# The state product of a chunked scan: one float32 matmul per chunk against three matmuls of two-part operands, issued in another order

## The chip, the cores and the metric

The kernel runs on one core of one Trainium2 chip. The metric is the device time of one launch in microseconds (us). Three runs of the kernel before took 2647.37, 2649.1 and 2652.85 us; the median is 2649.1 us.

## The reference

One layer of a hybrid trunk over 2048 positions of 1024 features: RMSNorm, one wide input projection, two token mixers (a gated short convolution, and a state-space mixer), an output projection with a residual, then a squared-ReLU MLP and a last RMSNorm. The change lies in the state-space mixer alone. It has 16 heads of 64 in 2 groups, and a state of 128 for each group. Cut to what matters, for one chunk of positions `l`, `s` and one group:

```python
a_cum = cumsum(dt * a_head)
y_diag = einsum(scores * exp(a_cum[l] - a_cum[s]), x * dt)        # inside the chunk
states = einsum("ln,lrp->rpn", b, x * dt * exp(a_cum[-1] - a_cum))   # what the chunk adds to the state
h0 = zeros
h_next = h * exp(a_cum[-1]) + states                               # from chunk to chunk
y_off = einsum("ln,rpn->lrp", c, h_before) * exp(a_cum)            # what the state adds to the chunk
y = y_diag + y_off
```

The first chunk reads a state of zeros, and the state after the last chunk is read by nobody. After it come a skip term (`d_skip * x`), a gate (`silu(z)`) and a grouped RMSNorm.

## The kernel before

All large products (input projection, output projection, MLP) are float32-like: each operand is split into two float32r parts, `hi` (ScalarE copies and rounds) and `lo` (VectorE subtracts), and a product is three matmuls, `hi*hi`, `hi*lo` and `lo*hi`, into one PSUM bank (`mm3`, lines 111 to 114, and the same three in `Seven.chain`, lines 269 to 271). The big projections use a two-by-two scheme of seven block products.

The scan (class `Scan`) uses chunks of 128 positions: 4 blocks of 512 positions, 2 groups, 4 chunks each, so 32 chunks in the order of `CHUNKS`. They are numbered 0 to 31 here; the first chunks of the two groups are 0 and 4, the last ones are 27 and 31. Its work is woven into two stages of large products: chunks 0 to 15 into the second half of the input projection (`Proj.second_half`, profile 480 to 980 us), chunks 16 to 31 into the output projection (`Output.unit`, profile 980 to 1290 us). Each chunk has a `front` and a `back`, both generators, and `run` (the one who sets the order in which the source issues them) takes pieces of `back(n)` and of `front(n + 1)` in turn, one piece at each hook of the large stage.

The front, in three pieces: TensorE transposes the four x tiles into a PSUM bank (`ptx`, line 1227) and B into another (`ptb`, line 1229), and multiplies B by C into the rest of that bank (line 1230). ScalarE copies them out (`xtok` line 1232, `btok` line 1234), and VectorE masks the scores (`smask`, line 1236). Then ScalarE makes the decay table `dec` of the chunk, eight Relu passes (line 1241), which wait for the load of `dec` from DRAM, and one Exp over 1024 columns (line 1242); four passes scale the x tiles by `d_skip` (`xd`, line 1244), and VectorE makes `xdt` and `xde`, x times dt and x times the decay to the end of the chunk (line 1247). Last, VectorE multiplies `dec` by the masked scores (line 1249).

The back: TensorE multiplies the state by C (`yo`, four matmuls, line 1261), then B by `xde` (`st`, one float32 matmul of 128 by 512, line 1263), then eight matmuls for the heads (`yd`, line 1266). VectorE updates the state (lines 1274, 1275), adds the parts (1277, 1278, 1281), gates (1282), and ScalarE and VectorE form the norm (1285 to 1296).

The order on each engine is not the source's alone: a scheduler reorders the instructions of all engines by readiness and by its own estimates when the kernel is built. The order rows further down are what it has made. Each engine works through its own list in that order, and all DMA of the kernel is issued from SyncE's list, in its order. The PSUM tag `tp` has two banks that `ptx`, `ptb`, `st` and, in the first of the two stages, the norm's sum take in turn. `yo` and `yd` have one bank each. The temporaries of 512 columns (`stmp`) come from a ring of 3 tiles in the first stage and 4 in the second; the tables `dec`, `xd` and the loads have one tile in the first stage and two in the second.

Of the kernel before, what the change touches and what calls it, by code (L numbers as in the profile page):

```python
# [11 lines left out]
F32 = mybir.dt.float32  # L12
F32R = mybir.dt.float32r
AF = mybir.ActivationFunctionType
ALU = mybir.AluOpType

P = 128
# [3 lines left out]
NB = T // TB  # L21
L = 128
# [17 lines left out]
def trunk(ctx: ExitStack, tc: tile.TileContext, x, w_in, w_dt, w_out, w_up, w_down, cvec, hrow, out):  # L40
# [70 lines left out]
    def mm3(out, whi, wlo, hi, lo, k, nk):  # L111
        nc.tensor.matmul(out, whi, hi, start=(k == 0), stop=False)  # L112
        nc.tensor.matmul(out, whi, lo, start=False, stop=False)  # L113
        nc.tensor.matmul(out, wlo, hi, start=False, stop=(k == nk - 1))  # L114

    def psum(tag, name, bufs=1):
        if tag in turns:
            tag, bufs = next(turns[tag])
        return ps.tile([P, 512], F32, tag=tag, name=name, bufs=bufs)
# [1029 lines left out]
    class Scan:  # L1149
        def __init__(self, pool):  # L1150
            self.state = []
            for g in range(G):
                s0 = pool.tile([P, 512], F32, name=f"state{g}")
                nc.vector.memset(s0, 0.0)
                self.state.append(s0)
# [9 lines left out]
        def tmp(self):  # L1165
            return self.tile([512], "stmp", 2 + self.bufs)
# [6 lines left out]
        def load(self, n):  # L1173
# [20 lines left out]
            t["a"] = dd[:, 1, r0 : r0 + HG]  # L1194

        def load_rows(self, n):

            if n >= self.end:
                return
            b, g, c, h, ts, r0 = self.place(n)  # L1200
            if self.bufs == 1:
                eb = self.tile([4, L], "eb", 1)
            else:

                eb = uh.tile([P, 1, TB], F32R, tag="uh3", name="eb", bufs=4).bitcast(F32)
                eb = eb[:, 0].rearrange("p (j l) -> p j l", j=4)
            self.got[n]["eb"] = eb
            for hf in range(2):
                src = rd_d[b][r0 : r0 + HG, 1, :].rearrange("(j t) l -> t j l", t=2)[hf]
                nc.sync.dma_start(eb[hf * 64 : (hf + 1) * 64], src.partition_broadcast(64))  # L1210
# [7 lines left out]

        def front(self, n):
# [9 lines left out]
            nc.tensor.transpose(pb[:, 0:P], bT, ident)  # L1229
# [3 lines left out]
            btok = t["btok"] = self.tile([P], "btok", 1)  # L1233
            nc.scalar.copy(btok, pb[:, 0:P])
            sm = self.tile([L], "smask", 1)
            nc.vector.tensor_tensor(out=sm, in0=pb[:, P : 2 * P], in1=tri, op=ALU.mult)
            yield
# [7 lines left out]
            for k, by in (("xdt", "dt"), ("xde", "dend")):  # L1245
                t[k] = self.tmp()
                nc.vector.tensor_tensor(out=byhead(t[k]), in0=byhead(xtok), in1=t[by], op=ALU.mult)
# [4 lines left out]
        def back(self, n):  # L1252
# [6 lines left out]
            yo = psum("yo", "yo")  # L1259
            for j in range(4):  # L1260
                nc.tensor.matmul(yo[:, j * L : (j + 1) * L], state[:, j * P : (j + 1) * P], cT, start=True, stop=True)  # L1261
            st = psum("tp", "st", 2)
            nc.tensor.matmul(st, t["btok"], t["xde"], start=True, stop=True)  # L1263
# [10 lines left out]
            nc.vector.tensor_tensor(out=byhead(state), in0=byhead(state), in1=t["cdec"], op=ALU.mult)  # L1274
            nc.vector.tensor_tensor(out=state, in0=state, in1=st, op=ALU.add)
            t1 = self.tmp()
            nc.vector.tensor_tensor(out=t1, in0=yo, in1=t["eb"].rearrange("p j l -> p (j l)"), op=ALU.mult)
            nc.vector.tensor_tensor(out=t1, in0=t1, in1=yd, op=ALU.add)
            yield
            t3 = t1.rearrange("p (j l) -> p j l", j=4)  # L1280
            nc.vector.tensor_tensor(out=t3, in0=t3, in1=t["xd"], op=ALU.add)
# [10 lines left out]
            r = self.tile([L], "srstd", 1)  # L1292
# [342 lines left out]
```

## Time and profile before

| what | value |
|---|---|
| median of three runs | 2649.1 us (2647.37 to 2652.85) |
| the profiled execution, its own time | 2645.76 us |
| its span in the trace | 2643.8 us |
| TensorE busy (matmul) | 2596.8 us, 98% |
| VectorE busy | 1944.1 us, 74% |
| ScalarE busy | 1423.3 us, 54% |
| mean granted clock of TensorE | 0.997 |
| mean busy share of the DMA engines, 980 to 1100 us | 0.91 |
| mean busy share of the DMA engines, 1100 to 1265 us | 0.74 |

Times in the trace are microseconds from the start of the span. A row of the timeline gives start, duration, engine, line, operation, the tiles written and read, the shapes, how many instructions are merged into the row, and in brackets the idle time of the engine just before it with what ended it. A float32 matmul is two records in the trace (`yo` shows as x8 for four matmuls, `st` as x2 for one). Matmuls overlap, so what one costs is read from the starts of its neighbours, not from its own duration. The profiled execution is 3.3 us shorter than the median, and its span lies 2.0 us inside its own time.

### The profile page before, as it was taken

The page shows a single profiled execution, that of the slowest core. Times are in us where ns is not written, and L with a number is a line of the kernel's source. Part 1 is how long each engine was busy: PE and PEld are TensorE (multiplying, and loading weights), DVE is VectorE, ACT ScalarE, POOL GpSimd, SP SyncE. Part 2 cuts the span into 40 slices and gives each one's busy share as a digit, 9 for nine tenths or more (in the row PEclk, how much of TensorE's full clock was granted, in tenths as well). Part 3 has the DMA queues.
Part 4 walks back from the last instruction along what each step waited for, and adds up shares of the span by engine and source line. Part 5 has one row for each costly group of instructions (what it writes and reads, how often), then busy time and mean ns, then how long its engine had stood idle before and what let it go on. Part 6 is the DMA issues. An engine that isn't in the chain of part 4 may idle for free.

```text
span 2643.8 us, 33439 instructions
## 1 busy us (share of the span) xinstructions
PE 2596.8 (98%) x12026; PEld 2122.1 (80%) x12026; DVE 1944.1 (74%) x2650; ACT 1423.3 (54%) x2150; POOL 54.2 (2%) x98
## 2 busy tenths in 40 slices
PE   7999999999999999999999999999999999999998
PEld 5778888778878888888888888788887888888887
DVE  7997676767777777768767765755558877888885
ACT  6644345777567666666326555655555444444443
POOL 0000010000000000000000000000000000000001
PEclk9999999999999999999999999999999999999999
DMA  3585344655555478967666674744448554665762
GB/s 146 189 300 193 138 149 169 212 157 167 160 170 181 153 243 272 290 208 229 211 209 213 234 271 139 260 158 143 163 148 287 162 150 149 212 207 181 238 206 70
DMA packets 284806, 511.78 MB, mean 194 GB/s; under 512 B 25312, under 2 KB 141024, under 8 KB 284640
## 3 DMA queue, kind: packets, MB, share of 16 engines
q1 hardware_dynamic: 284640, 509.65, 58.5%
q8 instruction: 94, 1.54, 0.2%
q14 instruction: 72, 0.59, 0.1%
HBM read 344.41 MB, written 165.15 MB: 193 GB/s over the span
## 4 chain that ended last, share of the span: by engine, by line
PE 65%; issue 25%; DVE 3%; DMA 3%; ACT 3%; SPq 0%; POOL 0%; POOLq 0%; DVEq 0%; ACTq 0%
PE px L269 9%; PE px L271 9%; PE px L270 9%; PE pm L112 5%; PE pm L113 5%; PE pm L114 5%; PE py L269 4%; PE py L271 4%; PE py L270 4%; PE pw L269 2%; PE pw L271 2%; PE pw L270 2%; PE yd L1266 1%; PE st L1263 1%; PE yo L1261 1%
## 5 line engine op out<-in xcount | busy, mean ns | idle before, releaser
L269 PE MATMUL px<-uh,whi 128*128 128x512 f32 x1672 | 656.7, 393 | 11.7 <-ACT pw L277 4.8
L271 PE MATMUL px<-uh,wlo 128*128 128x512 f32 x1672 | 651.8, 390 | 1.8 <-DVE wlo L104 1.8
L270 PE MATMUL px<-ul,whi 128*128 128x512 f32 x1672 | 651.5, 390 | 0.0
L104 DVE TENSOR_TENSOR wlo<-wraw,whi 128x1024 fp32r<-128x1024 f32 x230 | 233.6, 1016 | 205.5 <-ACT whi L103 199.3
L269 PEld LDWEIGHTS px<-uh,whi 128*128 128x128 f32 x1672 | 314.0, 188 | 86.5 <-ACT pw L277 7.8
L271 PEld LDWEIGHTS px<-uh,wlo 128*128 128x128 f32 x1672 | 314.1, 188 | 68.9 <-DVE wlo L104 2.7
L270 PEld LDWEIGHTS px<-ul,whi 128*128 128x128 f32 x1672 | 314.2, 188 | 63.5
L103 ACT CAST whi<-wraw 128x1024 fp32r<-128x1024 f32 x230 | 203.4, 885 | 276.3 <-PE px L270 188.0
L103 ACT CAST whi<-s 128x1024 fp32r<-128x1024 f32 x210 | 219.6, 1046 | 234.3 <-PE pw L270 77.7
L269 PE MATMUL py<-uh,whi 128*128 128x512 f32 x836 | 327.3, 392 | 1.8 <-DVE acc L986 1.4
L270 PE MATMUL py<-ul,whi 128*128 128x512 f32 x836 | 325.4, 389 | 0.0
L271 PE MATMUL py<-uh,wlo 128*128 128x512 f32 x836 | 325.3, 389 | 0.0
L104 DVE TENSOR_TENSOR wlo<-s,whi 128x1024 fp32r<-128x1024 f32 x210 | 255.4, 1216 | 84.9 <-ACT whi L103 81.7
L112 PE MATMUL pm<-uh,whi 128*128 128x512 f32 (+1 forms) x648 | 252.6, 391 | 2.1 <-ACT uh L204 2.1
L113 PE MATMUL pm<-ul,whi 128*128 128x512 f32 (+1 forms) x648 | 248.9, 384 | 0.0
L114 PE MATMUL pm<-uh,wlo 128*128 128x512 f32 (+1 forms) x648 | 248.4, 383 | 0.0
L269 PEld LDWEIGHTS py<-uh,whi 128*128 128x128 f32 x836 | 156.9, 188 | 36.1 <-DVE acc L986 1.8
L271 PEld LDWEIGHTS py<-uh,wlo 128*128 128x128 f32 x836 | 156.8, 188 | 32.9
L270 PEld LDWEIGHTS py<-ul,whi 128*128 128x128 f32 x836 | 157.0, 188 | 32.2 <-issue 0.2
L269 PE MATMUL pw<-uh,whi 128*128 128x512 f32 x418 | 163.6, 391 | 0.7 <-ACT pw L277 0.7
L270 PE MATMUL pw<-ul,whi 128*128 128x512 f32 x418 | 163.0, 390 | 0.0
L319 ACT CAST uh<-rh 128x1024 fp32r<-128x1024 f32 (+1 forms) x128 | 120.4, 944 | 78.9 <-PE py L271 62.4
(226 smaller groups left out, 3710.6 us busy)
## 6 DMA issues: line engine op xcount, KB each, us to landing
hid_d<-e SPq DMA_DIRECT2D x96, 512.0 KB, 3.7
rh<-hid_d SPq DMA_DIRECT2D x96, 512.0 KB, 4.4
wraw<-w_in SPq DMA_DIRECT2D x68, 512.0 KB, 4.1
wraw<-w_up SPq DMA_DIRECT2D x64, 512.0 KB, 4.4
wraw<-w_down SPq DMA_DIRECT2D x104, 256.0 KB, 3.7
dec<-rd_d SPq DMA_DIRECT2D x32, 512.0 KB, 5.7
wraw<-w_out SPq DMA_DIRECT2D x32, 512.0 KB, 5.4
x_d<-xt SPq DMA_DIRECT2D x64, 256.0 KB, 3.8
```

The source lines that it names most:

```text
L103: nc.scalar.copy(hi, raw)
L104: eng.tensor_tensor(out=lo, in0=raw, in1=hi.bitcast(F32), op=ALU.subtract)
L112: nc.tensor.matmul(out, whi, hi, start=(k == 0), stop=False)
L113: nc.tensor.matmul(out, whi, lo, start=False, stop=False)
L114: nc.tensor.matmul(out, wlo, hi, start=False, stop=(k == nk - 1))
L269: nc.tensor.matmul(p, hi, h[0], start=bool(first and k == 0), stop=False, **kw)
L270: nc.tensor.matmul(p, hi, h[1], start=False, stop=False, **kw)
L271: nc.tensor.matmul(p, lo, h[0], start=False, stop=(k == len(g) - 1), **kw)
L319: nc.scalar.copy(p[i][0], t)
L1261: nc.tensor.matmul(yo[:, j * L : (j + 1) * L], state[:, j * P : (j + 1) * P], cT, start=True, stop=True)
L1263: nc.tensor.matmul(st, t["btok"], t["xde"], start=True, stop=True)
L1266: nc.tensor.matmul(yd[(i % 2) * 64 : (i % 2) * 64 + 64, (i // 2) * L : (i // 2 + 1) * L], byhead(t["xdt"])[:, i, :], t["dec"][:, i, :], st ...
```

## The change

The state product becomes an `mm3` of two-part operands: `btok` and `xde` are now pairs of float32r tiles which a new helper `pieces` makes (ScalarE rounds, VectorE subtracts). Both pairs are made in the first piece of the front, and so is `xdt`; `xde` is now x scaled in place in `xtok`. In the back, the state product stands ahead of the product of the state itself. The first chunk of each group has no product with the zero state, no load of its decay rows `eb` and no zeroed state; it copies `st` into the state. The last chunk of each group has no state product, no transpose of B and no update of the state. The norm's `srstd` is written over `ssq`, and the ring of temporaries has one tile less.

```diff
         def __init__(self, pool):
             for g in range(G):
-                s0 = pool.tile([P, 512], F32, name=f"state{g}")
-                nc.vector.memset(s0, 0.0)
-                self.state.append(s0)
+                self.state.append(pool.tile([P, 512], F32, name=f"state{g}"))
...
-            return self.tile([512], "stmp", 2 + self.bufs)
+            return self.tile([512], "stmp", 1 + self.bufs)
...
+            t["first"], t["last"] = (b, c) == (0, 0), (b, c) == (NB - 1, NC - 1)
 
         def load_rows(self, n):
...
+            if self.got[n]["first"]:
+                return
...
+        def pieces(self, shape, tag, src):
+
+            pair = self.sp.tile([P] + shape, F32R, tag=tag, name=tag, bufs=1)
+            hi, lo = pair[:, 0], pair[:, 1]
+            nc.scalar.copy(hi, src)
+            nc.vector.tensor_tensor(out=lo, in0=src, in1=hi.bitcast(F32), op=ALU.subtract)
+            return hi, lo
 
         def front(self, n):
...
-            nc.tensor.transpose(pb[:, 0:P], bT, ident)
+            if not t["last"]:
+                nc.tensor.transpose(pb[:, 0:P], bT, ident)
             nc.tensor.matmul(pb[:, P : 2 * P], bT, cT, start=True, stop=True)
             xtok = self.tile([512], "xtok", 1)
             nc.scalar.copy(xtok, pt)
-            btok = t["btok"] = self.tile([P], "btok", 1)
-            nc.scalar.copy(btok, pb[:, 0:P])
+            if not t["last"]:
+                t["btok"] = self.pieces([2, P], "btok", pb[:, 0:P])
             sm = self.tile([L], "smask", 1)
             nc.vector.tensor_tensor(out=sm, in0=pb[:, P : 2 * P], in1=tri, op=ALU.mult)
+            t["xdt"] = self.tmp()
+            nc.vector.tensor_tensor(out=byhead(t["xdt"]), in0=byhead(xtok), in1=t["dt"], op=ALU.mult)
+            if not t["last"]:
+                nc.vector.tensor_tensor(out=byhead(xtok), in0=byhead(xtok), in1=t["dend"], op=ALU.mult)
+                t["xde"] = self.pieces([2, 512], "xde", xtok)
             yield
...
-            for k, by in (("xdt", "dt"), ("xde", "dend")):
-                t[k] = self.tmp()
-                nc.vector.tensor_tensor(out=byhead(t[k]), in0=byhead(xtok), in1=t[by], op=ALU.mult)
             yield
...
-            yo = psum("yo", "yo")
-            for j in range(4):
-                nc.tensor.matmul(yo[:, j * L : (j + 1) * L], state[:, j * P : (j + 1) * P], cT, start=True, stop=True)
-            st = psum("tp", "st", 2)
-            nc.tensor.matmul(st, t["btok"], t["xde"], start=True, stop=True)
+            if not t["last"]:
+                st = psum("tp", "st", 2)
+                mm3(st, *t["btok"], *t["xde"], 0, 1)
+            if not t["first"]:
+                yo = psum("yo", "yo")
+                for j in range(4):
+                    nc.tensor.matmul(yo[:, j * L : (j + 1) * L], state[:, j * P : (j + 1) * P], cT, start=True, stop=True)
             yd = psum("yd", "yd")
...
-            nc.vector.tensor_tensor(out=byhead(state), in0=byhead(state), in1=t["cdec"], op=ALU.mult)
-            nc.vector.tensor_tensor(out=state, in0=state, in1=st, op=ALU.add)
             t1 = self.tmp()
-            nc.vector.tensor_tensor(out=t1, in0=yo, in1=t["eb"].rearrange("p j l -> p (j l)"), op=ALU.mult)
-            nc.vector.tensor_tensor(out=t1, in0=t1, in1=yd, op=ALU.add)
-            yield
             t3 = t1.rearrange("p (j l) -> p j l", j=4)
-            nc.vector.tensor_tensor(out=t3, in0=t3, in1=t["xd"], op=ALU.add)
+            if t["first"]:
+                nc.vector.tensor_copy(state, st)
+                yield
+                nc.vector.tensor_tensor(out=t1, in0=yd, in1=t["xd"].rearrange("p j l -> p (j l)"), op=ALU.add)
+            else:
+                if not t["last"]:
+                    nc.vector.tensor_tensor(out=byhead(state), in0=byhead(state), in1=t["cdec"], op=ALU.mult)
+                    nc.vector.tensor_tensor(out=state, in0=state, in1=st, op=ALU.add)
+                nc.vector.tensor_tensor(out=t1, in0=yo, in1=t["eb"].rearrange("p j l -> p (j l)"), op=ALU.mult)
+                nc.vector.tensor_tensor(out=t1, in0=t1, in1=yd, op=ALU.add)
+                yield
+                nc.vector.tensor_tensor(out=t3, in0=t3, in1=t["xd"], op=ALU.add)
...
-            r = self.tile([L], "srstd", 1)
+            r = ssq
```

Counted over the whole program, TensorE has 90 float32r matmuls of 128 by 512 for `st` in the place of 32 float32 ones, 120 instead of 128 for `yo`, and 30 instead of 32 transposes of B. VectorE has 30 more subtractions of 128 columns and 30 more of 512, and lacks two zeroings, and two or four each of the state's and the output's passes. ScalarE has 30 more casts of 512 columns and 86 instead of 89 table loads. SyncE has four loads fewer. Ahead of chunk 0 and behind chunk 31 the lists of all engines read alike.

The state product on TensorE, in chunk 5 (`st` is the state product, `yo` the product with the state, `yd` the heads). Before:

```order
L1261 MATMUL yo<-bc,state_3779 128x128 x4
L1263 MATMUL st<-stmp,btok 128x512
L1266 MATMUL yd<-dec,stmp 64x128 x8
```

And now:

```order
L112 MATMUL st<-xde,btok 128x512
L113 MATMUL st<-xde,btok 128x512
L114 MATMUL st<-xde,btok 128x512
L1277 MATMUL yo<-bc,state_3778 128x128 x4
L1280 MATMUL yd<-dec,stmp 64x128 x8
```

The group stays at the same place between the large matmuls in all middle chunks; inside it, the state product has come to the front.

ScalarE around the front of chunk 26, in the output projection. `xtok` and `btok` are this chunk's, while the `dec` rows and the Exp with its table load (L1242 before, L1257 now) are already those of the chunk after it; `stmp<-y` is the square of the norm, `whi` a weight of the projection. Before:

```order
L1285 ACTIVATE stmp<-y 128x512
L1241 ACTIVATE dec<-dec,dd 128x128 x4
L1244 ACTIVATE xd<-xd,cv 128x128
L1232 COPY xtok<-ptx 128x512
L1234 COPY btok<-ptb 128x128
L1244 ACTIVATE xd<-xd,cv 128x128 x3
L1241 ACTIVATE dec<-dec,dd 128x128 x4
L1242 ACT_TABLE_LOAD
L1242 ACTIVATE dec<-dec 128x1024
L103 CAST whi<-wraw 128x1024
```

And now:

```order
L1256 ACTIVATE dec<-dec,dd 128x128 x8
L1259 ACTIVATE xd<-xd,cv 128x128 x2
L1242 COPY xtok<-ptx 128x512
L1224 CAST btok<-ptb 128x128
L1305 ACTIVATE stmp<-y 128x512
L1259 ACTIVATE xd<-xd,cv 128x128 x2
L1257 ACT_TABLE_LOAD
L1257 ACTIVATE dec<-dec 128x1024
L1224 CAST xde<-xtok 128x512
L103 CAST whi<-wraw 128x1024
```

All eight passes over `dec` now stand ahead of the copy `xtok`, and the cast `xde`, which is new, stands behind the square, the table load and the Exp. VectorE at the same place, now:

```order
L1248 TENSOR_TENSOR stmp<-xtok,dd 128x512
L1225 TENSOR_TENSOR btok<-ptb,btok 128x128
L1246 TENSOR_TENSOR smask<-ptb,tri 128x128
L1250 TENSOR_TENSOR xtok<-xtok,dd 128x512
L1306 TENSOR_TENSOR stmp<-stmp 128x256
L1261 TENSOR_TENSOR dec<-dec,smask 128x1024
L1308 TENSOR_TENSOR ssq<-stmp 128x128
L1225 TENSOR_TENSOR xde<-xtok,xde 128x512
L1481 TENSOR_TENSOR xt<-pm,xt 128x512
```

The subtraction `xde`, the last thing that the state product needs, stands behind the product of `dec` with the scores. In chunks 25, 26 and 29 the Exp of the next chunk stands ahead of the cast `xde`; in 23, 24 and 30 it stands behind it.

ScalarE ahead of the Exp of chunk 2, in the input projection. Before:

```order
L717 ACT_TABLE_LOAD
L717 ACTIVATE ea<-pw 128x512
L651 ACT_TABLE_LOAD
L651 ACTIVATE dts<-pr 64x128
L1232 COPY xtok<-ptx 128x512
L725 ACT_TABLE_LOAD
L725 ACTIVATE eb<-eb 128x512
L1234 COPY btok<-ptb 128x128
L1293 ACT_TABLE_LOAD
L1293 ACTIVATE srstd<-pss,cv 128x128
L731 ACT_TABLE_LOAD
L731 ACTIVATE ea<-ea 128x512
```

And now:

```order
L651 ACTIVATE dts<-pr 64x128
L1242 COPY xtok<-ptx 128x512
L1256 ACTIVATE dec<-dec,dd 128x128
L1224 CAST btok<-ptb 128x128
L1313 ACT_TABLE_LOAD
L1313 ACTIVATE ssq<-pss,cv 128x128
L725 ACT_TABLE_LOAD
L725 ACTIVATE eb<-eb 128x512
L1224 CAST xde<-xtok 128x512
L731 ACTIVATE ea<-ea 128x512
```

Three of the five table loads of this stretch are gone, since the passes that share a table now stand together; one pass over `dec` and the cast `xde` have come in.

## The prediction

> **What bounds the kernel now.** I read the page first, then the busy time by stretches, then the timeline of each engine around single chunks.
>
> ```profile
> PE 2596.8 (98%) x12026; PEld 2122.1 (80%) x12026; DVE 1944.1 (74%) x2650; ACT 1423.3 (54%) x2150; POOL 54.2 (2%) x98
> 1100.00:1265.00 165.00, 164.42 (x879) 132.51 (x878) 121.61 (x186) 100.50 (x198) 0.00 (x0) 1.00 0.74 226
> ```
>
> TensorE is the bound, and in the second scan stage, too (second row: 164.4 of 165 us busy, granted clock 1.00; VectorE 121.6, ScalarE 100.5). So every microsecond that TensorE need not work comes off the end, as long as nothing makes it stand. The first half of my sum is its work, the second half its standing.
>
> The work of one chunk stands between large matmuls. Chunk 4 has all three products, chunk 3 `st` and `yd` alone, chunk 12 `yo` and `st` alone:
>
> ```profile
> 611.46 0.39 PE L271 MATMUL py<-uh,wlo 128*128 128x512 f32 x1
> 611.69 1.05 PE L1261 MATMUL yo<-bc,state 128*128 128x128 f32 x8
> 612.58 1.02 PE L1263 MATMUL st<-stmp,btok 128*128 128x512 f32 x2
> 613.53 1.09 PE L1266 MATMUL yd<-dec,stmp 128*64 128x128 f32 x16
> 614.90 0.40 PE L270 MATMUL px<-ul,whi 128*128 128x512 f32 x1
> ...
> 583.78 0.40 PE L271 MATMUL pw<-uh,wlo 128*128 128x512 f32 x1
> 584.01 1.02 PE L1263 MATMUL st<-stmp,btok 128*128 128x512 f32 x2
> 586.32 0.39 PE L270 MATMUL px<-ul,whi 128*128 128x512 f32 x1
> ...
> 841.82 0.39 PE L271 MATMUL px<-uh,wlo 128*128 128x512 f32 x1
> 842.93 1.02 PE L1263 MATMUL st<-stmp,btok 128*128 128x512 f32 x2
> 844.02 0.40 PE L270 MATMUL py<-ul,whi 128*128 128x512 f32 x1
> ```
>
> A large float32r matmul takes 0.39 us by its own row, yet the next starts 0.23 us after it (611.46 to 611.69). Each group lies between two large matmuls with a third inside, so its cost is the distance from the first row to the last, less two times 0.23: 2.98 us for all three products, 2.08 for `st` and `yd`, 1.74 for `yo` and `st`. By differences `yo` costs 0.89 and `st` 0.85; by its start and the start behind it (612.58 to 613.53) `st` costs 0.95. These are the bounds, 0.85 and 0.95.
>
> **The change, part by part: TensorE's work.** Three float32r matmuls of the shape of the large ones cost 3 x 0.23 = 0.69 us. So a chunk saves 0.16 to 0.26 us, and 30 chunks 4.8 to 7.8 us; I take 6. Two first chunks lose `yo` (2 x 0.89 = 1.8), two last ones `st` (2 x 0.85 = 1.7) and a transpose each (an eighth of `yo`'s 0.89, so 0.2 together). Sum: 9.7 us, bounds 8.5 and 11.5.
>
> The Trainium skill ("FP8 and Floating Point Precision", TensorE Precision Notes) says that true float32 goes through the array in four passes, and the reduced form reads a truncated operand. By that rule `st` costs 4 x 0.23 = 0.91 us as an estimate, and the 30 chunks save 6.6 us instead of 6; the rows agree within their bounds.
>
> **A stall that goes.** In chunk 2 TensorE stands 1.66 us ahead of `yd`, because the Exp of the decay table is late on ScalarE:
>
> ```profile
> 552.14 1.28 ACT L1242 ACT_TABLE_LOAD   x1
> 553.44 1.06 ACT L1242 ACTIVATE dec<-dec 128x1024 f32<-128x1024 f32 x1
> ...
> 556.02 1.09 PE L1266 MATMUL yd<-dec,stmp 128*64 128x128 f32 x16 [1.66 <-DVE dec L1249]
> ```
>
> The new ScalarE list has three table loads fewer ahead of this Exp (3 x 1.28 = 3.8 us) and about 1 us of new passes, so the Exp comes 2.8 us sooner. I take 1.5 us of gain, bounds 0 and 1.7.
>
> **New waits on TensorE.** The state product now needs a longer chain: `xtok` copied (ScalarE), scaled (VectorE), rounded (ScalarE), subtracted (VectorE). It also stands first in its group, so the 0.89 us of `yo` no longer hide anything, and `yo`, `yd` and all large matmuls queue behind it. The Trainium skill ("PSUM — Partial Sum Buffer", Engine vs sequencer instructions) says the same of all lists: ScalarE and VectorE are strict first-in first-out, and matmuls start in order. By that rule a late part costs its full lateness; with overtaking it would cost nothing, and the sum would be 11.2 us of gain.
>
> In the input projection the chain has room: in chunk 12, the tightest of 4 to 15, `xde` is ready at 834.3, 7.7 us ahead of `yo` at 842.04 (0.89 ahead of the `st` above). In the output projection it has not, since ScalarE itself stands, waiting for the load of the next chunk's `dec` (seven times from 1100 to 1250 us). The rows are chunk 12's `xde`, that wait, and chunk 26:
>
> ```profile
> 833.60 0.68 DVE L1247 TENSOR_TENSOR stmp<-xtok,dd 128x512 f32<-128x512 f32 x1
> ...
> ACT dec L1241 <- DMA dec<-rd_d: 21.0, 7, 4.5
> ...
> 1160.81 1.28 ACT L1241 ACTIVATE dec<-dec,dd 128x128 f32<-128x128 f32 x4 [3.94 <-DMA dec<-rd_d]
> 1162.29 0.56 ACT L1232 COPY xtok<-ptx 128x512 f32<-128x512 f32 x1
> 1162.76 0.26 ACT L1234 COPY btok<-ptb 128x128 f32<-128x128 f32 x1
> 1162.91 0.99 ACT L1244 ACTIVATE xd<-xd,cv 128x128 f32<-128x128 f32 x3
> 1163.80 1.27 ACT L1241 ACTIVATE dec<-dec,dd 128x128 f32<-128x128 f32 x4
> 1165.09 1.28 ACT L1242 ACT_TABLE_LOAD   x1
> 1166.39 1.06 ACT L1242 ACTIVATE dec<-dec 128x1024 f32<-128x1024 f32 x1
> 1167.35 1.03 ACT L103 CAST whi<-wraw 128x1024 fp32r<-128x1024 f32 x1
> ...
> 1162.89 0.69 DVE L1247 TENSOR_TENSOR stmp<-xtok,dd 128x512 f32<-128x512 f32 x1 [4.56 <-ACT xtok L1232]
> 1163.50 0.28 DVE L1236 TENSOR_TENSOR smask<-ptb,tri 128x128 f32<-128x128 f32 x1
> 1163.70 0.68 DVE L1247 TENSOR_TENSOR stmp<-xtok,dd 128x512 f32<-128x512 f32 x1
> 1164.30 1.22 DVE L1249 TENSOR_TENSOR dec<-dec,smask 128x1024 f32<-128x1024 f32 x1
> ...
> 1166.28 1.05 PE L1261 MATMUL yo<-bc,state 128*128 128x128 f32 x8
> ```
>
> From start to start a `dec` or `xd` pass takes 0.30 us, a copy of 512 columns 0.47 (so I take the square and the cast at 0.5), `btok` 0.15, the table load 1.30, the Exp 0.96; on VectorE 0.60 for 512 columns, 0.20 for 128, 1.13 for 1024. The new list, from the landing at 1160.81: eight `dec` 2.4, two `xd` 0.6, `xtok` 0.5, `btok` 0.15, square 0.5, two `xd` 0.6, table 1.3, Exp 1.0, cast 0.5: the `hi` part is ready at 1168.4, `lo` 0.65 later at 1169.0. TensorE comes at 1166.28 and needs `lo` for its second matmul, 0.23 us on: it stands 2.5 us. The other four tight chunks go the same way from their own copy of `xtok`:
>
> ```profile
> 1125.04 0.56 ACT L1232 COPY xtok<-ptx 128x512 f32<-128x512 f32 x1
> 1128.20 1.05 PE L1261 MATMUL yo<-bc,state 128*128 128x128 f32 x8
> ...
> 1143.72 0.58 ACT L1232 COPY xtok<-ptx 128x512 f32<-128x512 f32 x1
> 1148.61 1.05 PE L1261 MATMUL yo<-bc,state 128*128 128x128 f32 x8
> ...
> 1220.49 0.56 ACT L1232 COPY xtok<-ptx 128x512 f32<-128x512 f32 x1
> 1222.05 1.05 PE L1261 MATMUL yo<-bc,state 128*128 128x128 f32 x8
> 1223.68 1.10 PE L1263 MATMUL st<-stmp,btok 128*128 128x512 f32 x2 [0.58 <-DVE stmp L1247]
> ...
> 1238.58 0.56 ACT L1232 COPY xtok<-ptx 128x512 f32<-128x512 f32 x1
> 1240.60 1.05 PE L1261 MATMUL yo<-bc,state 128*128 128x128 f32 x8
> ```
>
> In chunks 24 and 30 the Exp is behind the cast, and VectorE sets the end: from the end of the copy `xdt` 0.6, `btok` and `smask` 0.4, `xtok` 0.6, the half-sum 0.4, `dec` 1.13, the subtraction 0.65, in all 3.8: 0.9 us of standing in 24, 2.0 in 30. In chunk 25 nine `dec` and `xd` passes, square, table and Exp come first: 6.8 us from the copy's end, 2.2 us of standing. In chunk 29 it is 5.3 us, 4.0 of standing, of which 0.74 is there before (1222.05 + 0.89 to 1223.68): 3.3 new. Chunk 28 has the wait behind its copy, and 27 and 31 have no state product. Sum: 0.9 + 2.2 + 2.5 + 3.3 + 2.0 = 10.9 us, and 0.5 for chunks 0 and 16, whose products the list puts close behind their parts.
>
> Not all of it need come. While TensorE stands, SyncE's list and the transfers go on, so after a stall the next `dec` lands sooner as TensorE sees it; and the list has one load fewer ahead of some `dec` loads. I take 9 us, bounds 2 and 14 (above the sum, if VectorE's longer list makes the loads later).
>
> **What I cost at nothing.** The 30 x (0.2 + 0.6) us more on VectorE and 30 x 0.5 on ScalarE beyond these waits lie under TensorE (121.6 and 100.5 of 165 us busy); without that cover they would be 39 us. The state's update now waits for `yo` 0.69 us later on VectorE, under the same cover, since the next pass waits for `yd` anyway. The passes, loads and zeroing left out in first and last chunks gain as little. The smaller ring has each tile's last reader done ahead of its next writer.
>
> **Sum.** -9.7 - 1.5 + 9 = -2.2 us on the profiled span of 2643.8 us (2645.76 us by its own time, 3.3 under the median of 2649.1). On the median: 2646.9 us. Its own range, from the bounds: -11.5 - 1.7 + 2 = -11.2 to -8.5 + 14 = +5.5.
>
> **Rivals.** First, the waits do not come: the new order lets the `dec` loads land early enough that ScalarE no longer stands ahead of `xtok`. For it: SyncE's new list puts `dec` ahead of a load or store in three of these chunks. Against it: the wait is there seven times, 3.94 us in chunk 26. Then 0 to 3 us of waits are left: -11.2 + 2 = -9, 2640 us. Second, slower: VectorE, 0.8 us a chunk longer, evicts the units of the projection later, their stores go out later, and SyncE, in order, issues each `dec` that much later. This decides from about 0.5 us of delay a chunk on, and adds 0.8 us in each of six tight chunks (23 to 26, 29, 30) to the uncorrected 11.4: -11.2 + 11.4 + 4.8 = +5, or with chunk 28 drawn in +6: 2655 us. Third, the change does not do what it says: the matmuls of `st` take the 0.39 us of their rows each and not 0.23. Then `st` costs 1.17, 0.32 more than now, and the 30 chunks lose 9.6 us where I have a gain of 6: 2662.5 us. The large matmuls of the same shape, 0.23 apart, speak against it.
>
> **Chances.** The sum as it stands, 0.55 (2646.9); waits that mostly do not come, 0.30 (2640); late loads, 0.12 (2655); the third, 0.03 (2662.5). Two runs of this kernel differ by about 0.2%, 5.3 us, so that much is what a measurement can tell. Faster than 2643.8: most of the second case and a fifth of the first, 0.37. Slower than 2654.4: the last two and little of the first, 0.16. Between: 0.47. Range for 8 in 10: 2637 to 2654.
>
> **What would show it.** Right: `st` rows 0.23 apart at the head of each group and groups 0.16 to 0.26 us shorter; no wait at `yd` in chunk 2; TensorE standing 1 to 4 us ahead of the second or first `st` matmul in chunks 24, 25, 26, 29 and 30 with VectorE's `xde` as the releaser, and ScalarE waiting for `dec` ahead of `xtok`. Wrong: no standing there (then 2640), or standing in chunks 17 to 22 too, where I give 1.5 us of room and more.

## The result, and the profile after

The changed kernel took 2640.7 us (median of eight runs, 2636.3 to 2643.9); the kernel before, run beside it, 2647.5 us. The ratio is 0.998, with a 95% interval of 0.9971 to 0.9989: between 3 and 8 us faster, 5.3 us by the middle (the two medians lie 6.8 apart). The profiled execution took 2640.53 us, and its span went from 2643.8 to 2638.8 us. The forecast was 2646.9 us. The time lies inside the range, but at the number of my first rival, 2640; the range is wide enough to hold both.

The page's row of busy times, the stretch of the second scan stage by windows (start to end, length, then busy time of TensorE, its weight loads, VectorE, ScalarE and GpSimd, the granted clock, the DMA share and GB/s), and TensorE's waits from 470 to 1320 us (total, times, longest):

```profile
PE 2588.8 (98%) x12034; PEld 2127.0 (81%) x12034; DVE 1955.7 (74%) x2696; ACT 1432.9 (54%) x2175; POOL 58.2 (2%) x98
...
1100.00:1265.00 165.00, 161.90 (x872) 133.07 (x871) 122.66 (x195) 104.11 (x204) 0.00 (x0) 1.00 0.76 230
...
PE st L112 <- ACT xde L1224: 1.6, 2, 1.2
PE pss L1311 <- ACT xtok L1242: 1.5, 2, 0.7
PE ptx L1236 <- DMA xd<-xs_d: 1.4, 3, 0.6
PE st L113 <- DVE xde L1225: 1.3, 4, 0.6
```

TensorE works 8.0 us less in all, but in the second stage it is no longer busy throughout: it stood 0.58 us there before and 3.10 now. Two kinds of wait are new: `st` for the parts of `xde`, and the norm's sum `pss` for the copy of `xtok`.

A chunk without a wait, from TensorE's timeline (chunk 5):

```profile
636.94 0.40 PE L271 MATMUL px<-uh,wlo 128*128 128x512 f32 x1
637.17 0.39 PE L112 MATMUL st<-xde,btok 128*128 128x512 f32 x1
637.40 0.39 PE L113 MATMUL st<-xde,btok 128*128 128x512 f32 x1
637.63 0.40 PE L114 MATMUL st<-xde,btok 128*128 128x512 f32 x1
637.86 1.06 PE L1277 MATMUL yo<-bc,state 128*128 128x128 f32 x8
638.85 1.09 PE L1280 MATMUL yd<-dec,stmp 128*64 128x128 f32 x16
639.87 0.50 PE L269 MATMUL py<-uh,whi 128*128 128x512 f32 x1
640.20 0.39 PE L270 MATMUL py<-ul,whi 128*128 128x512 f32 x1
```

The three matmuls of the state product start 0.23 apart. From the first row to the last, less two times 0.227, the group costs 2.815 us; it was 2.979. Both are medians over the groups that hold these three products, so a chunk saves 0.164 us.

Chunk 25 is the longest wait. First TensorE, then ScalarE's list ahead of it:

```profile
1144.52 0.39 PE L114 MATMUL pm<-uh,wlo 128*128 128x512 f32 x1
1146.16 0.49 PE L112 MATMUL st<-xde,btok 128*128 128x512 f32 x1 [1.25 <-ACT xde L1224]
1146.88 0.50 PE L113 MATMUL st<-xde,btok 128*128 128x512 f32 x1 [0.23 <-DVE xde L1225]
```

```profile
1137.49 0.99 ACT L1256 ACTIVATE dec<-dec,dd 128x128 f32<-128x128 f32 x3 [6.65 <-DMA dec<-rd_d]
1138.39 1.03 ACT L103 CAST whi<-wraw 128x1024 fp32r<-128x1024 f32 x1
1139.32 0.58 ACT L1242 COPY xtok<-ptx 128x512 f32<-128x512 f32 x1
...
1142.25 0.98 ACT L1256 ACTIVATE dec<-dec,dd 128x128 f32<-128x128 f32 x3
1143.24 1.28 ACT L1257 ACT_TABLE_LOAD   x1
1144.54 1.06 ACT L1257 ACTIVATE dec<-dec 128x1024 f32<-128x1024 f32 x1
1145.50 0.60 ACT L1224 CAST xde<-xtok 128x512 fp32r<-128x512 f32 x1
```

ScalarE stands 6.65 us for the `dec` of chunk 26, while the copy of chunk 25's `xtok` stands behind it; then the rest of chunk 26's Relu passes, the table load and the Exp go ahead of the cast of `xde`. TensorE comes at 1144.75 and gets `hi` at 1146.1.

The kernel has 10,890 matmuls outside the scan, as many in every version. I set the k-th of one trace against the k-th of the other; the difference of their starts shows where time is won and lost. The whole gaps between them show waits more fully than the idle times in brackets: the stall of chunk 2 is 1.66 us in brackets and 2.1 by its gap. In us, against the kernel before (negative is earlier):

| place in the kernel before | the change |
|---|---|
| 468.6 us (scan not begun) | -0.8 |
| 563.9 us (chunk 2 done) | -4.5 |
| 971.8 us (first stage nearly done) | -3.7 |
| 1103.7 us (chunk 22 done) | -5.1 |
| 1159.0 us (chunk 25 done) | -2.0 |
| 1274.2 us (scan done) | -4.2 |
| 2633.4 us (end) | -4.6 |

So the scan is worth 3.4 us of the 5.0; the rest lies in stages that the change doesn't touch, where two executions of one kernel differ as much (experiments 5 and 11 run the same kernel; at 468.6 us one is 1.1 us ahead of the kernel before, the other 0.7 behind). The gains come at the first chunks and the last ones. Between chunk 2 and chunk 22 the cheaper products (20 x 0.164) and the `yo` that chunk 4 lacks (0.89) should give 4.2 us and leave 0.6: waits of `pss` take 2.0, chunk 3's `yo`, which stood ahead of the mark at 563.9 and now stands behind it, 0.9, and the other 0.7 is spread over waits of large products and transposes. Chunks 23 and 25 take 3.5.

### The profile page after: what moved, and what is told of

Read it like the earlier page. It is cut to its first block, busy times and chain, and to the rows that moved or that the text cites. A ratio compares the mean times of both kernels' runs of the same rounds, so it can differ in the third digit from the quotient of the medians.

```text
span 2638.8 us, 33504 instructions
## 1 busy us (share of the span) xinstructions
PE 2588.8 (98%) x12034; PEld 2127.0 (81%) x12034; DVE 1955.7 (74%) x2696; ACT 1432.9 (54%) x2175; POOL 58.2 (2%) x98
## 4 chain that ended last, share of the span: by engine, by line
PE 65%; issue 25%; DMA 4%; DVE 3%; ACT 3%; SPq 0%; POOL 0%; POOLq 0%; DVEq 0%; ACTq 0%
PE px L269 9%; PE px L271 9%; PE px L270 9%; PE py L269 5%; PE py L271 4%; PE py L270 4%; PE pm L112 4%; PE pm L113 4%; PE pm L114 4%; PE pw L269 2%; PE pw L271 2%; PE pw L270 2%; DMA dec<-rd_d 1%; PE yd L1280 1%; PE yo L1277 1%
## 5 line engine op out<-in xcount | busy, mean ns | idle before, releaser
L271 PE MATMUL pw<-uh,wlo 128*128 128x512 f32 x418 | 162.9, 390 | 0.0
```

The costliest lines, as they stand in the source:

```text
L271: nc.tensor.matmul(p, lo, h[0], start=False, stop=(k == len(g) - 1), **kw)
```

## The experiments

Theory A: the change saves about 8.6 us of TensorE's work and a stall of 1.66, and loses part of it because the parts of `xde` come late in the second stage, behind the next chunk's `dec` on ScalarE. Theory B: the two-part product is worth nothing here in any case, and the gain comes from the rest. The last five columns are the same differences of starts, in us, at the places of the table above:

| kernel | median us | ratio to before, 95% | 563.9 | 971.8 | 1103.7 | 1159.0 | 1274.2 |
|---|---|---|---|---|---|---|---|
| the change | 2640.7 | 0.998 (0.9971 to 0.9989) | -4.5 | -3.7 | -5.1 | -2.0 | -4.2 |
| 1 float32 product, first | 2641.9 | 0.9985 (0.9976 to 0.9994) | -4.7 | -4.0 | -3.1 | -3.1 | -5.9 |
| 2 state's own product first | 2646.9 | 1.0004 (0.9993 to 1.0016) | -0.3 | -2.5 | -3.0 | +0.6 | -2.5 |
| 4 ends only | 2645.4 | 0.9994 (0.9981 to 1.0007) | -0.9 | -1.1 | +0.4 | +0.6 | +2.3 |
| 5 Relu held behind | 2636.1 | 0.9959 (0.9945 to 0.9973) | -4.1 | -4.3 | -5.1 | -5.5 | -8.6 |
| 6 the same, float32 product | 2641.7 | 0.9989 (0.998 to 0.9999) | -5.4 | -5.1 | -1.7 | -1.4 | -4.2 |
| 7 parts late in the source | 2638.4 | 0.9977 (0.9968 to 0.9986) | -3.5 | -4.5 | -3.9 | -1.9 | -2.9 |

**1. The two-part operands undone alone.** `btok` and `xde` are plain float32 tiles, made at the same place:

```diff
-                t["btok"] = self.pieces([2, P], "btok", pb[:, 0:P])
+                btok = t["btok"] = self.tile([P], "btok", 1)
+                nc.scalar.copy(btok, pb[:, 0:P])
...
-                nc.vector.tensor_tensor(out=byhead(xtok), in0=byhead(xtok), in1=t["dend"], op=ALU.mult)
-                t["xde"] = self.pieces([2, 512], "xde", xtok)
+                t["xde"] = self.tile([512], "xde", 1)
+                nc.vector.tensor_tensor(out=byhead(t["xde"]), in0=byhead(xtok), in1=t["dend"], op=ALU.mult)
...
-                mm3(st, *t["btok"], *t["xde"], 0, 1)
+                nc.tensor.matmul(st, t["btok"], t["xde"], start=True, stop=True)
```

> The changed kernel with the two-part operands undone alone: the state product is one float32 matmul again, still first in its group, and xde and btok are plain float32 tiles made in the first piece. In the two traces a middle chunk went from 2.979 to 2.815 us, so 30 chunks should get 30 x 0.164 = 4.9 us longer. The chain ahead of the product gets shorter by a cast (0.5) and a subtraction (0.65). Theory A (the parts' lateness causes the new waits, 1.4, 1.9, 0.8 and 0.5 us in chunks 23, 25, 29 and 30): these 4.6 us mostly go, and the sum is 2640.7 + 4.9 - 4.6 = 2641, no difference from the changed kernel. Theory B (the waits come from the late decay load alone, whatever the operands are): the waits stay, 2645.6.

Measured: 2641.9 us, which the runs can't tell from the change. TensorE's timeline of chunk 5, and its one wait from 1090 to 1265 us:

```profile
635.57 1.02 PE L1274 MATMUL st<-xde,btok 128*128 128x512 f32 x2
636.43 1.05 PE L1278 MATMUL yo<-bc,state 128*128 128x128 f32 x8
637.41 1.09 PE L1281 MATMUL yd<-dec,stmp 128*64 128x128 f32 x16
...
PE ptb L1239 <- DVE state L1298: 1.0, 1, 1.0
```

Here `st` costs 0.86 us (635.57 to 636.43), and the groups have a median of 2.985 us. No wait at `st` is left, so the waits belong to the longer chain of the two-part operands, as A said. But the price stands too: as the change was built, the waits ate what the cheaper product saved (by the two traces the float32 version is even 1.7 us ahead at the end of the scan).

**2. The order undone alone.**

```diff
-            if not t["last"]:
-                st = psum("tp", "st", 2)
-                mm3(st, *t["btok"], *t["xde"], 0, 1)
             if not t["first"]:
                 yo = psum("yo", "yo")
...
+            if not t["last"]:
+                st = psum("tp", "st", 2)
+                mm3(st, *t["btok"], *t["xde"], 0, 1)
             yd = psum("yd", "yd")
```

> The changed kernel with the order undone alone: the product of the state stands ahead of the state product again. Theory A: its 0.89 us hide that much of each wait: 0.9 in chunks 23 and 25, 0.8 in 29, 0.5 in 30, so 3.1 us faster than the changed kernel, 2637.6. Rival: the float32r product between two float32 ones costs a switch that the large matmuls beside it hide in the changed order, up to 0.1 us at each of two places in 28 chunks, 5.6 us: then 2643, and groups of 2.9 to 3.0 us where they are 2.815.

Measured: 2646.9 us, 6 slower than the change, and for neither reason. The switch costs nothing: the groups have a median of 2.818 us. The waits at `st` in the second stage stay, since the list has become another one (chunks 23 and 24 stand longer than in the change, chunk 25 less). Most of the loss is in chunk 2: its gap is 3.7 us longer, 0.9 of it chunk 3's `yo`, which has moved in. TensorE, and the two ends of ScalarE's list there:

```profile
551.40 1.05 PE L1274 MATMUL yo<-bc,state 128*128 128x128 f32 x8
...
554.43 1.16 PE L1274 MATMUL yo<-bc,state 128*128 128x128 f32 x8 [1.28 <-DVE state L1297]
555.57 1.09 PE L1280 MATMUL yd<-dec,stmp 128*64 128x128 f32 x16
```

```profile
551.61 1.28 ACT L1257 ACT_TABLE_LOAD   x1
552.91 1.06 ACT L1257 ACTIVATE dec<-dec 128x1024 f32<-128x1024 f32 x1
```

The Exp is at 552.91 (548.57 in the change); from 537 us on seven table loads lead up to it, its own among them, not four. Now chunk 3's `yo` has been put ahead of chunk 2's `yd`, and waits for the state.

**3. The `dec` loads of the second stage issued from GpSimd.**

```diff
-            nc.sync.dma_start(t["dec"], rd_d[b][r0 : r0 + HG, 0, :].partition_broadcast(P))
+            if self.bufs == 1:
+                nc.sync.dma_start(t["dec"], rd_d[b][r0 : r0 + HG, 0, :].partition_broadcast(P))
+            else:
+                for i in range(0, HG, 4):
+                    nc.gpsimd.dma_start(t["dec"][:, i : i + 4], rd_d[b][r0 + i : r0 + i + 4, 0, :].partition_broadcast(P))
```

> The changed kernel with the loads of dec in the second scan stage issued from GpSimd, in two halves, and no longer from SyncE's list. Theory A (the new waits come from dec standing in SyncE's list behind loads and stores that wait for others): ScalarE no longer stands ahead of xtok (34.1 us in seven waits now), the 4.6 us of standing in chunks 23, 25, 29 and 30 go, 2636. Rival: the loads are late because the DMA engines are busy (0.76 to 0.90 of the time), so they land no sooner: 2640.7, and the waits stay. Second rival: the earlier transfers push others back: over 2642, with new waits for ry or wraw.

Measured: 2678.5 us, ratio 1.0135 (1.0116 to 1.0153): a miss for every theory, by 36 us and more. GpSimd's timeline, the row of these issues (number, size, median us to landing), and the waits from 470 to 1320 us (TensorE's, then ScalarE's from 980 us on):

```profile
1110.42 0.75 POOL L1192 DMA_DIRECT2D dec<-rd_d  x1 [12.54 <-PE pss L1315]
1118.41 0.75 POOL L1192 DMA_DIRECT2D dec<-rd_d  x1 [7.24 <-DVE wlo L104]
...
dec<-rd_d POOLq DMA_DIRECT2D x29, 256.0 KB, 5.3
...
PE st L112 <- ACT xde L1228: 18.0, 6, 5.9
...
ACT dec L1260 <- DMA dec<-rd_d: 83.1, 19, 10.9
```

The second half goes out only when the first has landed (in all 16 pairs 0.30 us after the landing, here 8 us after the first issue), so a table needs two transfers one after the other, and `dec` is later than from SyncE. The run says nothing for or against SyncE's list; it does show that a later `dec` comes out on TensorE as waits of `st`, up to 5.9 us each.

**4. The ends alone, on the kernel before.**

```diff
+            if not t["last"]:
                 nc.tensor.transpose(pb[:, 0:P], bT, ident)
...
+            if not t["first"]:
                 yo = psum("yo", "yo")
                 for j in range(4):
...
+            if not t["last"]:
                 st = psum("tp", "st", 2)
                 nc.tensor.matmul(st, t["btok"], t["xde"], start=True, stop=True)
...
+            if t["first"]:
+                nc.vector.tensor_copy(state, st)
```

> The kernel before with the first and last chunks' work left out alone: no product with the zero state, no decay rows for it, no state product, transpose or update in the last chunks; the float32 state product and its place stay. By the groups, 2.979 to 2.09 us without yo and to 2.117 without st: 2 x 0.89 + 2 x 0.86 = 3.5 us faster than the kernel before, 2644.0, if the stall of 1.66 us in chunk 2 stays; 2642.3 if it goes with the shorter lists of ScalarE. If more than this comes, a part of what I gave to the two-part product belongs here.

Measured: 2645.4 us against 2648.2 beside it; the interval holds both nothing and the 3.5 us. The groups did get shorter as expected (2.093 us without `yo`, 2.117 without `st`). Chunk 2's stall of 1.66 us is still there, again with seven table loads up to the Exp, so it did not go with the ends. This profiled execution (2649.6 us) stood 2.7 us for `st` in chunk 29, where the kernel before stands 0.6; so far as it goes, the ends are not the whole gain.

**5. Relu held behind the parts.** VectorE makes the bias of the next chunk's Relu passes out of this chunk's `hi` part, so those passes can't stand ahead of it:

```diff
+            if self.bufs == 2 and n + 1 < self.end:
+                ac = self.tile([HG], "acol")
+                src = xtok if t["last"] else t["xde"][0].bitcast(F32)
+                nc.vector.scalar_tensor_tensor(
+                    out=ac, in0=src[:, 0:HG], scalar=0.0, in1=self.got[n + 1]["a"], op0=ALU.mult, op1=ALU.add
+                )
+                self.got[n + 1]["a"] = ac
             yield
 
             dec = t["dec"]
```

> The changed kernel, with ScalarE's list held in order in the second scan stage: the Relu passes of chunk n + 1 read their bias from a small copy that VectorE makes from the hi part of chunk n's xde (times zero, plus the bias), so that they can't stand ahead of chunk n's xtok and xde in the list. No load, no buffer and no other operand differs. Theory A (the new waits come from ScalarE standing for the NEXT chunk's dec, whose buffer and whose place in SyncE's list make it late, with this chunk's xtok queued behind it): the waits of 1.4, 1.9, 0.8 and 0.5 us in chunks 23, 25, 29 and 30 go, 2640.7 - 4.6 = 2636. Rival: the decay table is then late itself, and TensorE stands ahead of yd in place of st: 2640 or more.

Measured: 2636.1 us, as A said. ScalarE in chunk 25, and TensorE's one wait from 1090 to 1265 us:

```profile
1132.48 0.58 ACT L1242 COPY xtok<-ptx 128x512 f32<-128x512 f32 x1
...
1136.66 0.62 ACT L1224 CAST xde<-xtok 128x512 fp32r<-128x512 f32 x1 [1.74 <-DVE xtok L1250]
1138.12 2.45 ACT L1263 ACTIVATE dec<-dec,acol 128x128 f32<-128x128 f32 x8 [0.84 <-DVE acol L1255]
...
PE st L113 <- DVE xde L1225: 0.2, 1, 0.2
```

The cast is ready at 1137.3, 6 us ahead of TensorE (1143.27), and the standing has gone: the scan ends 8.6 us ahead of the kernel before, 4.4 more than the change, where I had 4.6. The copy on VectorE costs 0.16 us. Nothing waits for `yd` in its place.

**6. The same with a float32 product.** The edits of 1 and 5 together.

> The kernel of the run before in this list with the state product as one float32 matmul (as in the first experiment). Theory A: without late parts on either side only the work is left, 0.17 us a chunk, 30 chunks: 5.1 us slower than with two-part operands, less the 2 us that two-part operands lost to two late pss in the first stage: 2636 + 3 to 5 = 2639 to 2641. Theory B (two-part operands are worth nothing here in any case): the same time as with two-part operands.

Measured: 2641.7 us, 5.6 slower than with two-part operands, just over A's upper end. The trace tells a less tidy story: 4.0 of it come from one stall ahead of 1103.7, which no theory had.

```profile
1098.86 0.33 PE L1239 MATMUL ptb<-ident,bc 128*128 128x128 f32 x1 [2.26 <-DVE state L1305]
...
1099.84 0.63 PE L113 MATMUL pm<-ul,whi 128*128 128x512 f32 x1
1100.27 0.63 PE L114 MATMUL pm<-uh,wlo 128*128 128x512 f32 x1
```

`ptb` takes a bank of the tag that `st` had, and the state's update had not read it yet. The gap itself is 2.6 us longer; the other 1.4 come behind it, where the granted clock is 0.51 from 1099.0 to 1102.4 us and the large matmuls start 0.43 apart instead of 0.23. Without this stall the two-part product would be worth 0.4 us by the traces at the end of the scan, about 5 by the groups' work (30 x 0.17). Of what lies between, 1.9 are waits of `pss` that only the two-part version has; the rest is spread over waits of the first stage, and I can't assign it. So what the two-part product is worth in all stays open.

**7. The parts made late in the source.** `xdt`, the scaled `xtok` and its pieces moved behind the decay table in `front`:

```diff
-            t["xdt"] = self.tmp()
-            nc.vector.tensor_tensor(out=byhead(t["xdt"]), in0=byhead(xtok), in1=t["dt"], op=ALU.mult)
-            if not t["last"]:
-                nc.vector.tensor_tensor(out=byhead(xtok), in0=byhead(xtok), in1=t["dend"], op=ALU.mult)
-                t["xde"] = self.pieces([2, 512], "xde", xtok)
             yield
...
                 nc.scalar.mul(t["xd"][:, j], t["xd"][:, j], col(C_D, 4 * g + j))
+            t["xdt"] = self.tmp()
+            nc.vector.tensor_tensor(out=byhead(t["xdt"]), in0=byhead(xtok), in1=t["dt"], op=ALU.mult)
+            if not t["last"]:
+                nc.vector.tensor_tensor(out=byhead(xtok), in0=byhead(xtok), in1=t["dend"], op=ALU.mult)
+                t["xde"] = self.pieces([2, 512], "xde", xtok)
```

> The changed kernel with the parts made last instead of first: xdt, the scaled xtok and the pieces of xde stand behind the decay table and the xd passes in the source, as xdt and xde did before. Theory A: where the list already holds ScalarE for the next dec, the parts of chunks 23 to 30 get behind eight Relu (2.4 us), the table load and the Exp (2.3 us) of their own chunk; each of six chunks stands up to 4 us longer, 2645 to 2660. If the place in the source says nothing (the order on each engine is made by readiness): 2640.7, the waits as they are.

Measured: 2638.4 us, no different from the change. TensorE's waits from 1090 to 1265 us have nearly the same sum (3.2 against 2.9), though not in the same chunks: chunk 25 stands 1.6 us less, chunk 30 0.9 more:

```profile
PE st L112 <- ACT xde L1224: 1.6, 2, 1.3
PE st L113 <- DVE xde L1225: 1.6, 4, 0.9
```

Making the parts first in a chunk is no part of the effect that these runs can tell. That readiness makes the list fits, but was not tested apart.

**8. The state product issued twice**, the second set starting anew:

```diff
                 mm3(st, *t["btok"], *t["xde"], 0, 1)
+                mm3(st, *t["btok"], *t["xde"], 0, 1)
```

> The changed kernel with the three float32r matmuls of the state product issued twice into the same bank (the second set starts anew, so the result is the same). Price of a float32r matmul of this shape by its neighbours' starts: 0.227 to 0.233, so 30 x 3 x 0.23 = 20.7 us more, 2661.4, if TensorE's work counts one to one. By the duration of their own rows, 0.39, it would be 35 us: 2676. Less than 20 would mean that standing hides some of it (the parts come sooner as TensorE sees them).

Measured: 2662.2 us, ratio 1.0063 (1.0045 to 1.0081); groups of 3.495 us, 0.680 more, so 0.227 for each matmul. 30 x 0.68 is 20.4 us, and the median (of three runs) rose by 21.5, so TensorE's work counts about one to one, and the 0.39 us of a matmul's own row is not its price. The sum is less clean than the groups: the profiled execution, the slowest of the three, lost 26.6 us in the scan, since chunks 24 and 29 stand longer for the parts than in the change.

**9. The hold of experiment 5 on the kernel before**, with `xtok` as its source:

```diff
+            if self.bufs == 2 and n + 1 < self.end:
+                ac = self.tile([HG], "acol")
+                src = xtok
...
+                self.got[n + 1]["a"] = ac
             yield
 
             dec = t["dec"]
```

> The kernel before, with the same hold on ScalarE's list in the second stage (the Relu passes of chunk n + 1 behind the copy of chunk n's xtok). Theory A: ScalarE's standing for the next dec (21 us there) costs the kernel before next to nothing, because its state product comes 0.89 us later and needs no cast and no subtraction; only the 0.6 us of chunk 29 can go: no difference from the kernel before, 2643 to 2648. If it gains 3 us or more, the hold is a gain of its own and says less on the two-part operands.

Measured: 2644.4 us, ratio 0.999 (0.9981 to 0.9999): at most 5 us, 2.6 by the middle, and 1 us between chunks 16 and 31 in the trace. Of that 1 us, 0.8 is the wait of chunk 29. So the hold alone is not the gain of experiment 5, whose ratio is worth 10.8 us (8.2 by the medians).

**10. The hold, and the state's own product first.** The edits of 2 and 5 together.

> The changed kernel with the hold on ScalarE's list and with the product of the state first again. Theory A: no wait for parts is left to cover in chunks 23 to 30, and the order costs TensorE nothing by itself (groups of 2.818 against 2.815), so what remains of the difference is chunk 2, where seven table loads stand ahead of the Exp again and the stall of 3.7 us returns: 2636 + 3.7 = 2640. If it is over 2643, the order costs something in other chunks.

Measured: 2641.4 us, 0.9982 (0.9972 to 0.9991), between the two expectations. Chunk 2's gap is 3.7 us longer than in the change, as expected (0.9 of it chunk 3's `yo`); chunk 29 loses 3.9 us, 1.9 of them standing, which was not.

```profile
PE st L112 <- ACT xde L1224: 1.9, 1, 1.9
PE yd L1287 <- DVE dec L1268: 0.3, 1, 0.3
```

The order has no price on TensorE; what experiments 2 and 10 lose by it lies in waits that come with another list.

**11. Experiment 5 once more.**

> The changed kernel with the hold on ScalarE's list once more, beside the two others on the same chip: 2636, 0.4% under the kernel before, again without standing at st in chunks 23 to 30.

Measured: 2636.7 us against 2645.7 beside it, 9.0 less; in experiment 5 it was 2636.1 against 2644.3, 8.2 less. The ratio and its interval (0.9959, 0.9945 to 0.9973) are the same for both, so they are one figure and not two. This version is faster than the kernel before. That it beats the change too is likely, not settled: the change's own interval (0.9971 to 0.9989) overlaps this one by 0.0002.

## Why the prediction was right or wrong

**What bounds the kernel.** Right: TensorE's work counts about one to one (experiment 8), and what it saves comes back only where nothing makes it stand.

**TensorE's work: mechanism right, 1.1 us too large.** I took 6 us for the 30 chunks between bounds of 4.8 and 7.8; the groups give 30 x 0.164 = 4.9, the low bound. The high one was no price of `st`: the start of `yd` comes 0.09 us late behind any product (`yo` to `yd` is 0.99 in chunk 5, not 0.89), so the 0.95 held a piece of `yd`. With the four products at the ends (3.5) and two transposes (0.2) the work is 8.6 us, not 9.7. The Trainium skill ("FP8 and Floating Point Precision", TensorE Precision Notes) gives true float32 four passes; by the 0.227 us that experiment 8 measured for one, that is an estimate of 0.91 us, and `st` took 0.86.

**The stall in chunk 2: right.** It went, for the reason given: the Exp now comes 4.9 us earlier (553.44 before, 548.57 now), with three table loads fewer ahead of it, and `yd` comes right behind `yo`.

```profile
547.27 1.28 ACT L1257 ACT_TABLE_LOAD   x1
548.57 1.06 ACT L1257 ACTIVATE dec<-dec 128x1024 f32<-128x1024 f32 x1
...
552.80 1.09 PE L1280 MATMUL yd<-dec,stmp 128*64 128x128 f32 x16
```

By the whole gap it was worth 2.1 us, more than my upper bound of 1.7, which I took from the brackets.

Experiment 1 lacks the stall too; 2, 4 and 10 keep seven table loads up to that Exp. Experiment 2 differs from the change in the order alone. So it is the state product's place that moved the list, by way of the scheduler, not the number of passes.

**The new waits: the step that failed.** I took 9 us (10.9 in chunks 24, 25, 26, 29 and 30, computed one by one, and corrected down). The gaps give 1.5 in chunk 23, 2.0 in 25, 0.9 in 29 and 0.5 in 30, and none in 24 and 26. Of the 0.9 in chunk 29, 0.8 is there before the change, so the new waits are 4.1 us. The mechanism was right: held behind, the Relu passes set `xtok` free and nearly all of the waits go (experiment 5), and a product without parts, in the same place, does not wait (1). What was wrong was a quantity that I carried over from the trace of before: how long ahead of TensorE the next `dec` lands. SyncE's issues around the `dec` of chunk 27, before and after, and ScalarE's first row behind its landing in the kernel after:

```profile
1153.27 0.44 SPq L98 DMA_DIRECT2D wraw<-w_out  x1
1153.82 0.38 SPq L1190 DMA_DIRECT2D dec<-rd_d  x1
```

```profile
1149.57 0.37 SPq L1188 DMA_DIRECT2D dec<-rd_d  x1
...
1153.53 0.71 SPq L98 DMA_DIRECT2D wraw<-w_out  x1
...
1155.10 2.45 ACT L1256 ACTIVATE dec<-dec,dd 128x128 f32<-128x128 f32 x8 [4.75 <-DMA dec<-rd_d]
```

Before, a load of 512 KB stands right ahead of it; after, it comes 4 us behind. The landing moves from 1160.8 to 1155.1, while TensorE's arrival moves only from 1166.28 to 1164.22: the table lands 9.1 us ahead, not 5.5, and the 2.5 us of standing that I had for chunk 26 are gone. In chunks 24, 25, 29 and 30 it lands 1.4, 0.5, 3.5 and 1.8 us earlier against TensorE, in chunk 23, which I had not listed, 1.1 us later. Taken off my own figures chunk by chunk, these shifts leave 0 in chunks 24 and 26, 1.7 in 25, 0.5 in 29 (before its old wait is taken off) and 0.2 in 30, close to what was measured. I had seen in SyncE's list that `dec` stands ahead of a load in three chunks, gave it as a reason to lower the sum, and lowered it by 2 us; the measured new waits are 6.8 us below it. That SyncE's order moved the landings is read from the two traces; no run here changed that order alone (experiment 3 meant to, and failed). Nor was it tested why one transfer took 6.97 us and the other 5.5 from issue to landing.

The strict order of the lists (the Trainium skill, "PSUM — Partial Sum Buffer", Engine vs sequencer instructions) agrees with this trace: `ptx` of chunk 25 is done by 1134, yet its copy starts only at 1139.32, behind the Relu passes and the cast, though ScalarE stood idle for 6.65 us up to 1137.49.

**What I cost at nothing: 2 us wrong.** In the first stage `pss` now waits twice for a bank that holds `ptx`, because the copy of `xtok` has moved back on ScalarE (in chunk 4 it starts 3.8 us behind the first transpose of `ptx`, 1.8 before); the two gaps are 2.0 us longer. Experiment 1, without the casts, has none of it. For chunks 0 and 16, which I gave 0.5, large matmuls fill the time between the three products, and nothing is lost.

**The sum** by these measured terms is -8.6 - 2.1 + 4.1 + 2.0 = -4.6 us, and the scan took 3.4 us less (-0.8 to -4.2 in the first table). The 1.2 us between lie in waits of large products and transposes that come and go from one execution to the next, and I can't assign them. That the scan's -3.4 lies near my -2.2 is in part luck: I had the waits 4.9 too large, while the work (1.1), the late `pss` (2.0) and those scattered waits (1.2) went the other way. Of the 6.2 us between forecast and time, 1.6 lie in the kernel before: I started from three runs with a median of 2649.1, where eight have 2647.5. **The rivals:** the first had the time (2640) and half the mechanism, earlier landings; but it left at most 3 us of waits, and 4.1 came. Of the second nothing came: no standing in chunks 17 to 22. Experiment 8 rules out the third.

## What to carry to other kernels

A cheaper product pays only as far as its operands are still early; count the longer chain of parts against the room at each place, and look at what stands ahead of it in the list of the engine that makes the parts. When a scheduler remakes the lists, don't carry a landing or a distance from the old trace into the new list: work out again, for each load, what stands ahead of it. And where one engine stands for data of the next step while this step's work queues behind it, a small false dependency that holds the order can be worth nearly as much as the change itself (here 4.4 us of the scan for 0.16 us of VectorE a chunk).

## What the runs showed of the hardware that was not expected

A float32r product between two float32 ones cost TensorE no switch: 2.818 us for the group against 2.815 with it beside large float32r matmuls. Two transfers of 256 KB issued from GpSimd for one tile ran one after the other, the second issued 0.30 us behind the landing of the first in all 16 pairs, where SyncE's single issue of 512 KB lands in 5 to 7 us.

A long wait of TensorE can cost more than itself. In experiments 4, 6 and 10, waits of 2.7, 2.3 and 1.9 us were followed, within 1.3 us of their end, by a stretch of 3.4 us at a granted clock of 0.5; in experiment 10 this makes a loss of 3.9 us out of a wait of 1.9. The length alone doesn't decide: the change stands 2.5 us at 1692.8 and 2.4 us at 2001.8, in a stage that it leaves alone, and only the first is followed by such a stretch.
